# A chain of layers on 256 tokens: constant products in the waits of TensorE, and a start with its side work moved behind the first block

## The chip, the cores and the metric

The kernel runs on one core of a Trainium2 chip, as one launch. The metric is the device time of that launch in microseconds (us). Of the kernel before, three runs took 2573.61, 2573.98 and 2575.96 us; the median, 2573.98 us, is the time before. Beside the runs there is one execution that the hardware profiler recorded; all durations below are from it.

The core has five engines, each with a queue of its own that is written when the program is built: TensorE (PE in the profile, with its weight loads shown apart as PEld), VectorE (DVE), ScalarE (ACT), GpSimd (POOL) and SyncE (SP, which here only starts transfers). Transfers (DMA) are issued from the queues of SP, POOL and ACT.

## The reference

`x` is 256 tokens of 2048 features. Two blocks follow each other. Everything is float32.

```python
def mixer_a(h, w_in, w_out):                     # first layer of the first block
    q, k, v, g = jnp.split(h @ w_in, 4, axis=-1)
    o = stick_breaking_attention(heads(q), heads(k), heads(v))
    return (o * jax.nn.silu(g)) @ w_out

def residual_update(x, out, g_post, p_i, w_pp, w_pg):
    x = x + rms_norm(out, g_post)
    return x + (p_i @ w_pp) * jax.nn.sigmoid(x @ w_pg)

# first_block: layer A as above, with h = rms_norm(x, norm_pre[0]), then a layer B with latent
# attention (keys and values from one normed 512-wide latent, queries from another)

def second_block(x, c, ...):
    mod = silu(c) @ w_ada + b_ada                # 2048 x 12288: "modulation"
    sh1, sc1, gt1, sh2, sc2, gt2 = jnp.split(mod[:, None, :], 6, axis=-1)
    h = rms_norm(x, g_pre_mix) * (1.0 + sc1) + sh1
    proj = h @ w_in                              # convolution branch, attention on chosen keys, gates
    ...
    x = x + gt1 * rms_norm(mixed @ w_o, g_post_mix)
    h = rms_norm(x, g_pre_ffn) * (1.0 + sc2) + sh2
    f = (silu(h @ w_gate) * (h @ w_up)) @ w_down
    return x + gt2 * rms_norm(f, g_post_ffn)
```

## The kernel before

**Blocks and units.** The program is one long row of blocks. A `Block` computes `act(t) @ w` for up to 512 columns of a weight matrix, for both halves t0 and t1 of the tokens (128 each), in a PSUM tile per half. Its weights come in pieces: a piece is one 128-row chunk in the first block and two in nearly all others. One piece against one half of the tokens is a unit; the emission clock of the program, `u`, counts units. The float32 product is made of three float32r products per chunk: L268 (high part of the weights times high part of the activations), L269 (low part of the weights) and L270 (low part of the activations).

**The weight stream.** SP starts the transfer of each piece into one of 4 staging buffers `wst` (L122 to L132). `consume` splits it: ACT copies it to `wh` (L148), DVE makes `wl`, the remainder (L149). `wh` and `wl` have 6 ring slots; a slot is free when both halves have met the piece, and a staging buffer when its `wl` is made. Pieces are emitted some units ahead of their first product.

**Side work.** Everything else (transposing and splitting activations, norms, attention, what reads a finished sum) is in generators that `side` (L225) advances between units; `yield n` lets n units pass. This fixes the order of each engine's queue when the program is built.

**The start** (`begin_a`, L510). SP loads `ident` and the eight quarters of x between the first weight pieces. PE transposes the gain vector (`rows0`, L542), ACT copies it (`pre0`, L543). `prep` then feeds x: per 512 features of a half, four PE transposes (L363), four ACT copies with the gain (`ah`, L371), four DVE remainders (`al`, L373). The norm of x is not applied to x; `norms` sums the squares of each half (four squares, L409 on ACT, then a total on DVE, L404), POOL makes the reciprocal root (L395, L397, copies in L560 and L561: `ra`, `rqa`), and what reads a finished sum scales by it. Block q0 (the first 512 query columns) is followed by block k0. When a half of q0 is summed, `heads_t` copies it from PSUM with that scale (`nat`, L603, on ACT), PE transposes it two units later (L610) and ACT copies it out (L611). In the same stretch `rest` copies constants on DVE, transposes tables of vectors on PE (L576, L577, L587) and makes `silu_c` on ACT (L580); ACT loads an activation table there and again in L590.

**Modulation.** The 2048 x 12288 product for one row is summed on DVE in 384 chunks of 128 x 512: POOL starts the transfer of a chunk (`ast`, L245), DVE multiplies and adds (L421, L424). `spread` (L1519) gives each chunk its unit: evenly over the "calm" units, away from the turns between phases. In the kernel before they begin at unit 30.

**The turn to the second block** (`to_c`, `affine`, L1047). A quarter of a half of x at a time: normed rows (`wide`, L1091, DVE), four PE transposes (L1056), scale and shift (L1064 on DVE or L1066 on ACT), the split (`ah` L1069 on ACT, `al` L1070 on DVE). The last block of the layer before fills the time between: its t1 units (tile `sc`) stand between the transposes of t0's first and second quarter. `to_f` (from L1387, norm in L1407) does the same for the feed-forward part, through the same `affine`.

**The end.** DVE makes the last eight tiles of the output (L1480) and SP starts their transfers (L1481).

Of the kernel before, what the change touches and what calls it, by code (L numbers as in the profile page):

```python
# [16 lines left out]
AF = mybir.ActivationFunctionType  # L17
# [5 lines left out]
P = 128  # L23
# [24 lines left out]
# columns of the table of row vectors, 128 values each  # L48
# [4 lines left out]
class Act:  # L53
    """A left operand, transposed and split: hi(t, kc) + lo(t, kc) are [128 features, 128 tokens].
    `done[t]` counts the chunks of 128 features that are emitted, `gens[t]` emit the rest."""
# [7 lines left out]
class Block:  # L63
    """acc[t] = act(t) @ w[kr, c0 : c0 + n] for both halves of the tokens, then epi(t, acc[t]).
    The weights come in `np` pieces of `cp` chunks of 128 rows; `groups`: how many pieces meet one
    half of the tokens before the other; `ahead`: a pool for the first `n_ahead` pieces, which are
    then split earlier than the ring allows."""
# [22 lines left out]
class Run:  # L90
    """Weights stream in pieces of several 128-row chunks, split into two float32r parts ahead of
    the matmuls; side work is emitted between the matmuls."""
# [28 lines left out]
    # ---- the weight stream  # L121
# [57 lines left out]
    # ---- side work  # L179
# [69 lines left out]
    def go(self):  # L249
        nc = self.nc  # L250
        for b in self.blocks:
# [4 lines left out]
            for t, i in b.units():  # L256
# [17 lines left out]
                if i == b.np - 1:  # L274
# [4 lines left out]
                    # what reads the sum is emitted right behind it  # L279
# [10 lines left out]
def body(ctx, tc, a, out):  # L290
# [7 lines left out]
    # ---------------------------------------------------------------- constants and row vectors  # L298
# [38 lines left out]
    def full_act(second=False):  # L337
        """A left operand of 16 chunks; its tiles come with the first of them."""
# [12 lines left out]
    def pair_act(tiles):  # L351
        """A left operand in two tiles [128, chunks, 256 tokens]."""
# [5 lines left out]
    def feed(act, t, kc0, src, scale=None):  # L358
        """Transposes [tokens, m * 128] into chunks kc0.. of `act`; `scale`: a gain per feature."""
# [9 lines left out]
        else:  # L369
            for c in range(m):  # L370
                nc.scalar.activation(hi[:, c, :], v[:, c, :], AF.Copy, scale=scale(kc0 + c))  # L371
# [5 lines left out]
    def feed_both(act, kc0, src):  # L377
        """The same for both halves of the tokens: src[t] [tokens, 256]."""
# [13 lines left out]
    def rstd_of(pool, ss, n, post=None):  # L392
        """(ss / n + eps) ** -0.5, times `post`."""
# [17 lines left out]
    # ---------------------------------------------------------------- modulation, a bit at a time  # L411
# [49 lines left out]
    extra_pool = {}  # L461

    class Phase:
        """A pool that holds one phase's tiles."""

        def __init__(self):
            self.pool = None
# [1115 lines left out]
```

## Time and profile before

| what | value |
|---|---|
| median of 3 runs | 2573.98 us (2573.61 to 2575.96) |
| the profiled execution: its span | 2573.5 us, 0.5 us under the median |
| PE busy in the span | 2530.5 us |
| DVE, ACT, POOL busy | 1689.0, 1262.0, 291.8 us |
| moved by DMA | 562.39 MB, 219 GB/s in the mean |
| modulation chunks | 384 transfers of 256 KB, DVE 746 ns for one |

The page of the profile gives, for each engine, the time in which it executed something; registers, branches, semaphores and DMA issues are not counted. PE is busy nearly all the time, so the stretches in which it is not are what can be gained, and every instruction that is put into its queue where it would not have waited is what can be lost. In a timeline row the columns are the start, the duration, engine, line, operation, output and inputs, shapes and count; in brackets stands how long the engine sat idle before the instruction, and who released it. Merged rows ("x4") stand for several like instructions in a row.

### The profile page before, as it was taken

The page shows a single profiled execution, that of the slowest core. Times are in us where ns is not written, and L with a number is a line of the kernel's source. Part 1 is how long each engine was busy: PE and PEld are TensorE (multiplying, and loading weights), DVE is VectorE, ACT ScalarE, POOL GpSimd, SP SyncE. Part 2 cuts the span into 40 slices and gives each one's busy share as a digit, 9 for nine tenths or more (in the row PEclk, how much of TensorE's full clock was granted, in tenths as well). Part 3 has the DMA queues.
Part 4 walks back from the last instruction along what each step waited for, and adds up shares of the span by engine and source line. Part 5 has one row for each costly group of instructions (what it writes and reads, how often), then busy time and mean ns, then how long its engine had stood idle before and what let it go on. Part 6 is the DMA issues. An engine that isn't in the chain of part 4 may idle for free.

```text
span 2573.5 us, 33331 instructions
## 1 busy us (share of the span) xinstructions
PE 2530.5 (98%) x12127; PEld 2101.4 (82%) x12127; DVE 1689.0 (66%) x2304; ACT 1262.0 (49%) x1814; POOL 291.8 (11%) x561
## 2 busy tenths in 40 slices
PE   8999999999999999999999999999999999999998
PEld 6888888878889978878877877888788888888886
DVE  6666667677775566668889756676765555645545
ACT  6544464455656545554444554445544444334443
POOL 2111112111313310000000001110100100100000
PEclk9999999999999999999999999999999999999999
DMA  8777768867886566655655535875577777756553
GB/s 266 248 254 250 237 227 283 286 199 247 283 285 191 188 227 208 222 191 174 188 160 168 172 138 181 279 281 197 185 263 232 237 234 233 246 181 188 192 192 127
DMA packets 271844, 562.39 MB, mean 219 GB/s; under 512 B 20800, under 2 KB 43584, under 8 KB 269632
## 3 DMA queue, kind: packets, MB, share of 16 engines
q1 hardware_dynamic: 237264, 439.61, 52.7%
q0 software_dynamic: 34384, 120.65, 13.5%
q8 instruction: 95, 1.56, 0.2%
q14 instruction: 69, 0.57, 0.1%
q10 hardware_dynamic: 32, 0.01, 0.0%
HBM read 551.79 MB, written 8.39 MB: 218 GB/s over the span
## 4 chain that ended last, share of the span: by engine, by line
PE 93%; DVE 4%; ACT 2%; issue 1%; DMA 1%; POOL 0%; DVEq 0%; POOLq 0%; ACTq 0%; SPq 0%
PE acc L268 21%; PE acc L270 21%; PE acc L269 21%; PE sc L268 7%; PE sc L270 7%; PE sc L269 7%; PE tp L363 1%; DVE wl L149 1%; PE sc L634 1%; PE sc L984 1%; PE tp L435 1%; PE sc L1274 1%; PE sc L1240 1%; PE pv L1274 0%; PE tp L610 0%
## 5 line engine op out<-in xcount | busy, mean ns | idle before, releaser
L149 DVE TENSOR_TENSOR wl<-wst,wh 128x1024 fp32r<-128x1024 f32 (+3 forms) x794 | 949.4, 1199 | 628.7 <-ACT wh L148 627.0
L148 ACT ACTIVATE wh<-wst 128x1024 fp32r<-128x1024 f32 (+3 forms) x794 | 822.5, 1039 | 852.5 <-PE sc L270 491.2
L268 PE MATMUL acc<-wh,ah 128*128 128x512 f32 (+4 forms) x1934 | 761.5, 394 | 7.7 <-ACT wh L148 3.7
L269 PE MATMUL acc<-wl,ah 128*128 128x512 f32 (+4 forms) x1934 | 744.6, 385 | 0.9 <-DVE wl L149 0.9
L270 PE MATMUL acc<-wh,al 128*128 128x512 f32 (+4 forms) x1934 | 744.9, 385 | 0.0
L268 PEld LDWEIGHTS acc<-wh,ah 128*128 128x128 f32 x1934 | 365.1, 189 | 81.5 <-issue 6.7
L270 PEld LDWEIGHTS acc<-wh,al 128*128 128x128 f32 x1934 | 364.5, 188 | 72.3 <-DVE al L389 0.9
L269 PEld LDWEIGHTS acc<-wl,ah 128*128 128x128 f32 x1934 | 365.2, 189 | 67.3 <-DVE wl L149 2.5
L245 POOL DMA_DIRECT2D ast<-in_w_ada_dram x384 | 209.3, 545 | 1579.1 <-DVE ada L424 1391.8
L424 DVE SCALAR_TENSOR_TENSOR ada<-ast,silu_c,ada 128x512 f32<-128x512 f32 x360 | 268.7, 746 | 41.3 <-DMA ast<-in_w_ada_dram 40.5
L268 PE MATMUL sc<-wh,ah 128*128 128x512 f32 x538 | 211.5, 393 | 0.0
L270 PE MATMUL sc<-wh,al 128*128 128x512 f32 x538 | 209.6, 390 | 0.0
L269 PE MATMUL sc<-wl,ah 128*128 128x512 f32 x538 | 209.4, 389 | 0.0
L270 PEld LDWEIGHTS sc<-wh,al 128*128 128x128 f32 x538 | 101.0, 188 | 21.4
L268 PEld LDWEIGHTS sc<-wh,ah 128*128 128x128 f32 x538 | 101.0, 188 | 20.5
L269 PEld LDWEIGHTS sc<-wl,ah 128*128 128x128 f32 x538 | 101.1, 188 | 20.3
L1145 DVE SCALAR_TENSOR_TENSOR cv<-cv,wdw 128x255 f32<-128x255 f32 (+14 forms) x240 | 112.4, 468 | 6.5
L153 ACT ACTIVATE wh<-wst,cols 128x512 fp32r<-128x512 f32 (+2 forms) x112 | 68.5, 664 | 47.5 <-PE acc L270 30.5
L154 DVE SCALAR_TENSOR_TENSOR wl<-wst,cols,wh 128x512 fp32r<-128x512 f32 (+2 forms) x112 | 71.3, 681 | 25.5 <-ACT wh L153 25.3
L268 PE MATMUL acc<-wh,hh 128*128 128x512 f32 x176 | 69.3, 393 | 0.0
L268 PE MATMUL sc<-wh,hh 128*128 128x512 f32 x176 | 69.1, 392 | 0.0
L270 PE MATMUL acc<-wh,hl 128*128 128x512 f32 x176 | 68.6, 390 | 0.0
(354 smaller groups left out, 2899.1 us busy)
## 6 DMA issues: line engine op xcount, KB each, us to landing
ast<-in_w_ada_dram POOLq DMA_DIRECT2D x384, 256.0 KB, 4.2
wst<-in_w_in_dram SPq DMA_DIRECT2D x144, 512.0 KB, 3.6
wst<-in_w_in_a_dram SPq DMA_DIRECT2D x120, 512.0 KB, 4.4
wst<-in_w_gate_dram SPq DMA_DIRECT2D x88, 512.0 KB, 4.3
wst<-in_w_up_dram SPq DMA_DIRECT2D x88, 512.0 KB, 4.2
wst<-in_w_down_dram SPq DMA_DIRECT2D x88, 512.0 KB, 4.1
wst<-in_w_ple_gate_dram SPq DMA_DIRECT2D x64, 512.0 KB, 4.8
wst<-in_w_in_b_dram SPq DMA_DIRECT2D x40, 512.0 KB, 4.6
```

What stands on the lines that cost most here:

```text
L148: nc.scalar.activation(wh, st, AF.Copy)
L149: nc.vector.tensor_sub(wl, st, wh.bitcast(F32))
L153: nc.scalar.activation(wh[:, c, :], st[:, c, :], AF.Copy, scale=g)
L154: nc.vector.scalar_tensor_tensor(wl[:, c, :], st[:, c, :], g, wh[:, c, :].bitcast(F32), op0=ALU.mult, op1=ALU.subtract)
L245: self.nc.gpsimd.dma_start(st, x[1])
L268: nc.tensor.matmul(o, lhsT=hi, rhs=wh[:, c, :], start=kc == 0, stop=False)
L269: nc.tensor.matmul(o, lhsT=hi, rhs=wl[:, c, :], start=False, stop=False)
L270: nc.tensor.matmul(o, lhsT=lo, rhs=wh[:, c, :], start=False, stop=kc == b.cp * b.np - 1)
L363: nc.tensor.transpose(tp[:, c * P : (c + 1) * P], src[:, c * P : (c + 1) * P], ident)
L424: nc.vector.scalar_tensor_tensor(acc, w, s, acc, op0=ALU.mult, op1=ALU.add)
L435: nc.tensor.matmul(tp[:, c : c + 1], lhsT=acc[:, c * P : (c + 1) * P], rhs=ones, start=c == 0, stop=True, skip_group_check=True)
L1145: nc.vector.scalar_tensor_tensor(acc[:, sft:], u[:, : S - sft], wdw[:, c, k : k + 1], acc[:, sft:], op0=ALU.mult, op1=ALU.add)
```

## The change

Five things.

1. `warm(n)` puts n products of the constant matrix `mean_c` with itself (128 x 128, float32) in PE's queue, into a PSUM tile that nothing reads. There are 47: 4 + 3 + 4 around the first transposes, 10 + 6 around the first transposes of t0 in `to_c`, 10 before the first transposes of each half in `to_f`. The memset of `mean_c` on DVE moves to the top of `begin_a` for it.
2. The copy of the gain vector (`pre0`) and the first four `ah` copies move from ACT to DVE.
3. `norms` begins at unit 31 or 32 in place of 14 or 15, with one unit between squares in place of two; `rest` begins at unit 42 in place of 12. Blocks q0 and k0 sum t1 in `sc` tiles (`spare=True`) in place of `acc`, and what reads q0 waits until its scale is emitted.
4. The modulation's chunks begin at unit 140 in place of 30: the same 384 chunks on fewer units.
5. Of the last eight output transfers, the even ones go to ACT's queue.

Comments are gone too, which shifts line numbers behind L290 (feed: L370, L381, L383; `nat` L620 and its transposes L627; squares L419, total L414, `ra`/`rqa` L575/L576; `affine`'s transposes L1075).

```diff
-    def feed(act, t, kc0, src, scale=None):
+    def warm(n):
+        spin = psum_v()
+        for _ in range(n):
+            nc.tensor.matmul(spin[:, :P], lhsT=mean_c, rhs=mean_c, start=True, stop=True)
+
+    def feed(act, t, kc0, src, scale=None, first=False):
...
             for c in range(m):
-                nc.scalar.activation(hi[:, c, :], v[:, c, :], AF.Copy, scale=scale(kc0 + c))
+                if first:
+                    nc.vector.tensor_scalar(hi[:, c, :], v[:, c, :], scale(kc0 + c), None, op0=ALU.mult)
+                else:
+                    nc.scalar.activation(hi[:, c, :], v[:, c, :], AF.Copy, scale=scale(kc0 + c))
...
     def begin_a():
         st["nb"], st["hb"], st["o"] = 4, 2, None
+        nc.vector.memset(mean_c, 1.0 / 1024)
...
-        nc.vector.memset(mean_c, 1.0 / 1024)
+        warm(4)
         tp = psum_t()
         nc.tensor.transpose(tp[:, :16], rows0, ident[:16, :16])
-        nc.scalar.activation(pre0, tp[:, :16], AF.Copy)
+        nc.vector.tensor_copy(pre0, tp[:, :16])
+        warm(3)
...
-                    feed(actA, t, 4 * g, x_nat[t][...], lambda k: pre0[:, k : k + 1])
+                    feed(actA, t, 4 * g, x_nat[t][...], lambda k: pre0[:, k : k + 1],
+                         first=g == 0 and t == 0)
+                    if g == 0 and t == 0:
+                        warm(4)
...
-            yield 14 + t
+            yield 31 + t
             for g in range(4):
                 square(x_nat[t][:, g * NB : (g + 1) * NB], parts[:, g : g + 1])
-                yield 2
+                yield 1
...
         def rest():
-            yield 12
+            yield 42
...
         def epi(t, acc):
+            while t not in st["r"]:
+                yield 1
...
         add_block(wa, (0, D), j * NB, NB, actA, heads_t("qT", ...),
-                  **(dict(before=begin_a, groups=[4] * 4, cp=1, lead=4) if j == 0 else {}))
-        add_block(wa, (0, D), D + j * NB, NB, actA, heads_t("kT", ...))
+                  **(dict(before=begin_a, groups=[4] * 4, cp=1, lead=4, spare=True) if j == 0 else {}))
+        add_block(wa, (0, D), D + j * NB, NB, actA, heads_t("kT", ...), spare=j == 0)
...
         for g in range(4):
+            if g == 0 and (i or t == 0):
+                warm(10)
             tp = psum_t()
             for c in range(4):
                 nc.tensor.transpose(tp[:, c * P : (c + 1) * P], xn[g][:, c * P : (c + 1) * P], ident)
+            if g == 0 and t == i == 0:
+                warm(6)
...
-                    nc.sync.dma_start(out[0, t * P : (t + 1) * P, s2], f[:, s2])
+                    q = nc.sync if g % 2 else nc.scalar
+                    q.dma_start(out[0, t * P : (t + 1) * P, s2], f[:, s2])
...
-        for qs, us in ((range(20), calm(30, uc - 30) + calm(uc + 300, uf - 30)), (range(20, 24), calm(uf + 40, uf + 300))):
+        for qs, us in ((range(20), calm(140, uc - 30) + calm(uc + 300, uf - 30)), (range(20, 24), calm(uf + 40, uf + 300))):
```

**ACT's queue around the first norms.** In the kernel before the squares (L409) stand between the pieces of block q0 (128x512), and the last of them ahead of q0's last two pieces; the copy of q0's sum for t0 (`nat`, L603) stands behind the second piece of k0 (128x1024). This is the end of that stretch:

```order
L409 ACTIVATE junk_445,xss4_176<-wide_96 128x512
L148 ACTIVATE wh_447<-wst_340 128x512
L148 ACTIVATE wh_466<-wst_351 128x512
L148 ACTIVATE wh_472<-wst_407 128x1024
L148 ACTIVATE wh_491<-wst_427 128x1024
L603 ACTIVATE nat_509<-acc_130,rqa1_457 128x512
L148 ACTIVATE wh_515<-wst_451 128x1024
```

Now the squares (L419) stand among the last pieces of k0. Call k0's eight pieces k0.0 to k0.7. The first square of t0 follows k0.4; from the next row on, `wh_486` is k0.5, `wh_514` is k0.6 and `wh_551` is k0.7. `xss4_189` collects the sums of t0, `xss4_190` those of t1:

```order
L148 ACTIVATE wh_486<-wst_440 128x1024
L419 ACTIVATE junk_499,xss4_189<-wide_96 128x512
L419 ACTIVATE junk_501,xss4_190<-wide_97 128x512
L419 ACTIVATE junk_510,xss4_189<-wide_96 128x512
L419 ACTIVATE junk_512,xss4_190<-wide_97 128x512
L148 ACTIVATE wh_514<-wst_461 128x1024
L419 ACTIVATE junk_526,xss4_189<-wide_96 128x512
L419 ACTIVATE junk_528,xss4_190<-wide_97 128x512
L419 ACTIVATE junk_546,xss4_190<-wide_97 128x512
L620 ACTIVATE nat_548<-acc_139,rqa1_537 128x512
L148 ACTIVATE wh_551<-wst_470 128x1024
L620 ACTIVATE nat_573<-sc_235,rqa1_564 128x512
```

The fourth square of t0 is `junk_526`, behind k0.6, and the copy of q0's t1 (`nat_573`) stands behind k0.7. On DVE the total of t0 stands behind the `wl` of k0.6 and that of t1 behind the `wl` of k0.7.

**PE's queue where q0's first transposes stand.** Before, they stand in block q0 itself, two units behind the end of its t0 half (the second group, of t1, follows in k0, 18 products later):

```order
L269 MATMUL acc_221<-wl_424,ah_185 128x512
L270 MATMUL acc_221<-wh_423,al_186 128x512
L610 MATMUL tp_524<-ident_68,nat_509 128x128 x4
L268 MATMUL acc_221<-wh_447,ah_185 128x512
L269 MATMUL acc_221<-wl_448,ah_185 128x512
L270 MATMUL acc_221<-wh_447,al_186 128x512
```

Now they stand in block k0, between its third and fourth piece (`wh_457`, `wh_466`):

```order
L270 MATMUL sc_503<-wh_457,al_200 128x512
L627 MATMUL tp_581<-ident_68,nat_548 128x128 x4
L268 MATMUL acc_492<-wh_466,ah_145 128x512
L269 MATMUL acc_492<-wl_467,ah_145 128x512
L270 MATMUL acc_492<-wh_466,al_146 128x512
L268 MATMUL acc_492<-wh_466,ah_145 128x512
L269 MATMUL acc_492<-wl_467,ah_145 128x512
L270 MATMUL acc_492<-wh_466,al_146 128x512
L627 MATMUL tp_599<-ident_68,nat_573 128x128 x4
L268 MATMUL sc_503<-wh_466,ah_199 128x512
```

Counted in products (L268 to L270) from the start of the program, the two groups of four transposes stood behind 90 and 108 of them and now stand behind 132 and 138. The products themselves are the same, in the same order.

**PE's queue at `to_c`.** Before, the first transposes follow the second to last t1 pieces of the layer before directly:

```order
L269 MATMUL sc_9952<-wl_9938,ah_9355 128x512
L270 MATMUL sc_9952<-wh_9937,al_9356 128x512
L1056 MATMUL tp_10085<-ident_68,wide_10046 128x128 x4
L268 MATMUL sc_9952<-wh_9961,ah_9355 128x512
L269 MATMUL sc_9952<-wl_9962,ah_9355 128x512
```

Now 10 constant products stand ahead of them and 6 behind:

```order
L269 MATMUL sc_9920<-wl_9906,ah_9296 128x512
L270 MATMUL sc_9920<-wh_9905,al_9297 128x512
L362 MATMUL pv_10053<-mean_c_76 128x128 x10
L1075 MATMUL tp_10064<-ident_68,wide_10014 128x128 x4
L362 MATMUL pv_10069<-mean_c_76 128x128 x6
L268 MATMUL sc_9920<-wh_9929,ah_9296 128x512
L269 MATMUL sc_9920<-wl_9930,ah_9296 128x512
```

The 12 products that follow, the transposes of the second quarter behind them and the first products of the second block are as before.

More of the change, by code (lines that the diff above doesn't have):

```diff
@@ L548, in prep @@
                 for t in range(2):
-                    feed(actA, t, 4 * g, x_nat[t][:, g * NB : (g + 1) * NB], lambda k: pre0[:, k : k + 1])
+                    feed(actA, t, 4 * g, x_nat[t][:, g * NB : (g + 1) * NB], lambda k: pre0[:, k : k + 1],
+                         first=g == 0 and t == 0)
+                    if g == 0 and t == 0:
+                        warm(4)
                     yield PREP[2 * g + t]
@@ L699, in body @@
         add_block(wa, (0, D), j * NB, NB, actA, heads_t("qT", ("qT", j), lambda t: st["rq"][t]),
-                  **(dict(before=begin_a, groups=[4] * 4, cp=1, lead=4) if j == 0 else {}))
-        add_block(wa, (0, D), D + j * NB, NB, actA, heads_t("kT", ("kT", j), lambda t: st["r"][t]))
+                  **(dict(before=begin_a, groups=[4] * 4, cp=1, lead=4, spare=True) if j == 0 else {}))
+        add_block(wa, (0, D), D + j * NB, NB, actA, heads_t("kT", ("kT", j), lambda t: st["r"][t]), spare=j == 0)
         add_block(wa, (0, D), 2 * D + j * NB, NB, actA,
```

## The prediction

> **What bounds the kernel now.** I read the page first: the busy times and the chain that ended last.
>
> ```profile
> span 2573.5 us, 33331 instructions
> ...
> PE 2530.5 (98%) x12127; PEld 2101.4 (82%) x12127; DVE 1689.0 (66%) x2304; ACT 1262.0 (49%) x1814; POOL 291.8 (11%) x561
> ...
> PE 93%; DVE 4%; ACT 2%; issue 1%; DMA 1%; POOL 0%; DVEq 0%; POOLq 0%; ACTq 0%; SPq 0%
> ```
>
> PE is the bound: it stands still for 43 us of 2573.5 (2573.5 - 2530.5), and all other engines matter only where PE waits for them. So a change can gain little but those 43 us and stretches at a low clock, and what is put into PE's queue costs its own time unless PE would have stood still there. I then looked for stretches of 50 us with little PE time, with the view by windows. Its columns are PE, PEld, DVE, ACT, POOL (instructions in brackets), the granted clock, the DMA share and GB/s.
>
> ```profile
> 0.00:50.00 50.00, 40.65 (x172) 30.48 (x173) 29.23 (x69) 36.64 (x82) 16.18 (x33) 0.97 0.77 245
> 1100.00:1150.00 50.00, 46.40 (x207) 37.02 (x207) 32.78 (x48) 27.78 (x42) 2.03 (x4) 0.97 0.58 188
> 1800.00:1850.00 50.00, 44.05 (x195) 35.25 (x194) 36.24 (x59) 32.70 (x60) 5.20 (x14) 0.93 0.41 132
> ```
>
> These are the start (9.35 us idle), the turn at `to_c` (3.6) and that at `to_f` (5.95), the three places of the change; in each the clock fell too. I went through PE's timeline in each.
>
> **The start.** PE's rows there; brackets hold the idle time before and its releaser. I count products (L268 to L270) from the first at 7.15; the row at 44.08 is the 97th, that at 54.07 the 139th.
>
> ```profile
> 8.39 0.80 PE L269 MATMUL acc<-wl,ah 128*128 128x512 f32 x1 [0.45 <-DVE wl L149]
> ...
> 9.84 0.63 PE L269 MATMUL acc<-wl,ah 128*128 128x512 f32 x1
> ...
> 13.68 0.46 PE L270 MATMUL acc<-wh,al 128*128 128x512 f32 x1
> ...
> 23.34 0.63 PE L363 MATMUL tp<-ident,wide 128*128 128x128 f32 x4 [0.59 <-DVE cols L578]
> ...
> 25.95 0.43 PE L587 MATMUL tp<-ident,nat 31*128 31x31 f32 x4
> ...
> 34.76 0.50 PE L268 MATMUL acc<-wh,ah 128*128 128x512 f32 x1 [1.20 <-ACT wh L148]
> ...
> 36.92 0.50 PE L268 MATMUL acc<-wh,ah 128*128 128x512 f32 x1 [0.70 <-ACT wh L148]
> 37.65 0.78 PE L269 MATMUL acc<-wl,ah 128*128 128x512 f32 x1 [0.23 <-DVE wl L149]
> ...
> 44.08 0.39 PE L268 MATMUL acc<-wh,ah 128*128 128x512 f32 x1
> ...
> 54.07 0.39 PE L268 MATMUL acc<-wh,ah 128*128 128x512 f32 x1
> ```
>
> From 44.08 to 54.07 PE starts 42 products and four transposes (0.35 us) without a wait: 0.23 us each. Until 13.68 they are 0.43 apart, so PE is at half its clock, and so again for some 3.4 us from 37.65 on. What the change takes from this stretch, against 0.23 a product: 2.65 us of low clock up to 13.68, if the constant products wake PE; about 4.0 us of waits (23.34, 34.76 to 37.65, with the late starts around them), since ACT is rid of the squares, of two table loads and `pre0`, DVE of the copies in `rest`, and the three modulation transfers leave the weights' way; the low clock behind 37.65, 1.7 us; and 1.5 us of transposes, which move behind: a group as at 25.95 takes 0.35 us of PE's time, and there are three of `rest`'s tables (1.05) and q0's first. Together 9.85, so the 97th product comes at about 34.2.
>
> The same norms now have to be ready later in the program but earlier in time. The rows of ACT that give the prices:
>
> ```profile
> 25.54 0.64 ACT L409 ACTIVATE junk<-wide 128x512 bf16<-128x512 f32 x1
> 26.06 0.21 ACT L409 ACTIVATION_READ_ACCUMULATOR junk<-wide 128x1 f32 x1
> ...
> 39.02 1.06 ACT L148 ACTIVATE wh<-wst 128x1024 fp32r<-128x1024 f32 x1 [0.69 <-DMA wst<-in_w_in_a_dram]
> ...
> 41.47 0.69 ACT L603 ACTIVATE nat<-acc,rqa 128x512 f32<-128x512 f32 x1 [1.39 <-POOL rqa L561]
> ```
>
> POOL's part of the norm, first half and second half, and what DVE did beside the first:
>
> ```profile
> 37.76 0.55 POOL L395 TENSOR_SCALAR var<-sst 128x1 f32<-128x1 f32 x1 [24.73 <-DVE sst L404]
> 38.40 1.62 POOL L397 TENSOR_TENSOR rstd<-var,mhalf 128x1 f32<-128x1 f32 x1
> ...
> 40.34 1.09 POOL L561 TENSOR_SCALAR rqa<-rstd 128x1 f32<-128x1 f32 x1
> 41.52 0.19 POOL L395 TENSOR_SCALAR var<-sst 128x1 f32<-128x1 f32 x1
> 41.79 0.57 POOL L397 TENSOR_TENSOR rstd<-var,mhalf 128x1 f32<-128x1 f32 x1
> ...
> 42.68 0.22 POOL L561 TENSOR_SCALAR rqa<-rstd 128x1 f32<-128x1 f32 x1
> ```
> ```profile
> 37.58 2.01 DVE L149 TENSOR_TENSOR wl<-wst,wh 128x512 fp32r<-128x512 f32 x2
> ...
> 40.11 1.23 DVE L149 TENSOR_TENSOR wl<-wst,wh 128x1024 fp32r<-128x1024 f32 x1 [0.46 <-ACT wh L148]
> ```
>
> From 37.76 to 41.43 the first takes 3.7 us, beside DVE's remainders; the second takes 1.4 (41.52 to 42.90) with DVE idle. And the weights:
>
> ```profile
> wst<-in_w_in_a_dram SPq DMA_DIRECT2D x7, 512.0 KB, 4.4
> ```
>
> A transfer of k0's pieces takes 4.4 us. Now the new order. The `wl` of k0.0 ends at 41.34 before (40.11 + 1.23), some 9.9 earlier now: 31.4. That frees the staging buffer for k0.4, which lands 4.4 later with a little issue time, at about 36.2. ACT then works through its queue, in which the squares stand behind it: `wh` k0.4 to 37.3, a square (0.75 with its read) to 38.0, `wh` k0.5 to 39.1, four squares to 42.1, `wh` k0.6 to 43.2, the last square of t0 to 43.9. DVE's remainder of k0.6 ends at 44.4, the total at 44.5, POOL's part 1.4 later (DVE's next remainder is of k0.7, whose `wh` stands behind `nat`) at 45.9, `nat` at 46.6. PE has finished the 132 products ahead of q0's transposes at 34.2 + 36 x 0.23 = 42.5. **A new wait of about 4 us.** The second half follows: `wh` k0.7 to 47.6, its remainder to 48.8, total 48.9, POOL 50.3, `nat` 51.0, transposes, and the 139th product at 51.4 in place of 54.07: 2.7 us gained. Given back behind it: the tables' transposes of `rest`, 1.05 us, and a low clock after 4 us of standing still, 1.7 us as behind 37.65. **The start comes to 0.** Its bounds: -3 (no low clock) to +4 (k0.4 lands 1 us later, or DVE's remainders slow POOL once).
>
> Should the constant products not wake PE, it reaches the transposes 2.65 us later and waits so much less; the start stays at 0.
>
> **`to_c`.** First the price of a constant product, from the row of like shape (three products, f32 128x128, shown as six records), then the turn:
>
> ```profile
> 103.44 0.83 PE L634 MATMUL pv<-v,w 128*128 128x128 f32 x6
> 104.02 0.48 PE L268 MATMUL acc<-wh,ah 128*128 128x512 f32 x1
> ```
> ```profile
> 1097.98 0.60 PE L1056 MATMUL tp<-ident,wide 128*128 128x128 f32 x4
> ...
> 1106.86 0.66 PE L1056 MATMUL tp<-ident,wide 128*128 128x128 f32 x4 [2.32 <-DVE wide L1091]
> 1108.80 0.50 PE L268 MATMUL acc<-awh,ah 128*128 128x512 f32 x1 [1.28 <-ACT ah L1069]
> ```
>
> Three take 0.58 us, so one 0.193. The first transposes at 1097.98 wait for nothing. Ten products ahead of them put them off by 1.93 us, and with them the chain that ends in the waits of 1106.86 and 1108.80, since ACT and DVE there work on what these transposes give. The six behind them, 1.16 us, fit into the wait of 2.32. I take **+1.93**. Bounds: +3.1 (the six cost too) and +0.2, if PE keeps its clock: the trace has a low clock for 3.4 us behind 1108.80, 1.7 us dearer. Nearest to what is left of the waits, 1.2 and 1.28 us around the transposes, are the waits from 34.76 to 37.65 (1.20, 0.70 and 0.23 among them), after which the clock fell; so I let it fall.
>
> **`to_f`.** Two groups of ten:
>
> ```profile
> 1810.72 0.63 PE L1056 MATMUL tp<-ident,nat 128*128 128x128 f32 x4 [1.94 <-DVE nat L1407]
> ...
> 1829.59 0.60 PE L1056 MATMUL tp<-ident,nat 128*128 128x128 f32 x4
> ```
>
> Ahead of t0's transposes PE waits 1.94 us, and ten products take 1.93: 0, at most +1.9 if DVE is earlier there. Ahead of t1's it waits for nothing: **+1.93**, at least 0 if a later wait takes it up.
>
> **The rest.** The modulation's chunks come closer together:
>
> ```profile
> L245 POOL DMA_DIRECT2D ast<-in_w_ada_dram x384 | 209.3, 545 | 1579.1 <-DVE ada L424 1391.8
> L424 DVE SCALAR_TENSOR_TENSOR ada<-ast,silu_c,ada 128x512 f32<-128x512 f32 x360 | 268.7, 746 | 41.3 <-DMA ast<-in_w_ada_dram 40.5
> ```
> ```profile
> 300.00:600.00 300.00, 297.62 (x1401) 246.33 (x1400) 208.70 (x247) 154.92 (x195) 46.37 (x86) 1.00 0.75 254
> ```
>
> Some 85 of 384 chunks fall into these 300 us (POOL's 46.37 by 0.545). On fewer units the program's table puts 0.68 of a chunk on a calm unit in place of 0.55, a quarter more; 21 more chunks add 21 x 0.746 = 16 us to DVE's 208.7 and 5.5 MB to 254 GB/s (272): both keep room, and PE loses 2.4 us there in all. I cost it at 0; if that cover goes, the waits on `wl` might double a few times, +4. `spare` only changes the tile that is summed into: 0. The last transfers:
>
> ```profile
> 2564.91 2.32 SPq L1481 DMA_DIRECT2D out_dram<-wide  x4
> ```
>
> Four issues in 2.32 us, the rate at which DVE makes the tiles; the last waits for DVE, not for a queue: 0, within 0.3 either way.
>
> **Sum.** 0 + 1.93 + 0 + 1.93 + 0 = +3.9 us on the profiled span of 2573.5: 2577.4. The median of the runs lies 0.5 above that span, so the time forecast is 2577.9.
>
> **Rivals.** *The norms come later still (slower).* POOL takes 3.7 us as at 37.76 in place of 1.4, for both halves, and each adds its 2.3 to the wait, since the second half's piece k0.7 stands behind the first half's `nat`: +4.6, in all +8.5, 2582.5. It decides at whether DVE makes a remainder while POOL works. For it speaks the first norm of before, against it that the new order leaves DVE nothing to make there. The Trainium skill ("SBUF — State Buffer", on port contention) says that a DVE operation with two SBUF inputs and a GpSimd operation that reads SBUF exclude each other; the two norms above agree (1.62 against 0.57 us for the same operation), and by it the forecast's quick norm holds as long as DVE stands still.
>
> *No new wait (faster).* Were k0's pieces and the squares some 4 us earlier for t0 and t1, the start would keep its 9.85 less 1.05: -8.8, in all -4.9, 2569.1, and down to 2567.4 with a clock that holds at `to_c`. For it speaks that the squares need nothing but x, and that the first ran at 25.54 before; against it ACT's strict order: they stand behind k0.4, which has no staging buffer before 31.4.
>
> *PE keeps its clock at `to_c`.* The stretch without ordinary products shrinks there from 4.3 us (1106.86 - 2.32 = 1104.5, to 1108.80) to 3.1: -1.7, in all +2.2, 2576.2. The Trainium skill ("TensorE: Matmul & The Clock Gate", Part 1) has the clock fall after an idle window of about 3.4 us, and its Part 4 says that transposes don't count as busy in the same way; by that the 4.3 us of before had to lower the clock and 3.1 would not. The trace agrees at `to_c`, but the fall at 37.65 came with no gap over 1.4 us, against the rule, which is why I don't take it as likeliest.
>
> **Chances.** The forecast 0.42, later norms 0.20, no new wait 0.20, the clock held 0.18. A measurement can tell 0.2% of this kernel, 5.1 us, from no change. Faster by more: most of "no new wait" and a little of the clock's case, 0.20. Slower by more: "later norms" and a third of the forecast, whose 3.9 lies near the border, 0.34. Within: 0.46. The range goes from 2567.4, where nothing waits, to 2585, where the norms are late and part of the modulation's 4 us comes too.
>
> **What would show it.** In the changed kernel's profile: products 0.23 us apart from about 9 us on; the 97th near 34; a wait of 3 to 5 us at the transposes of L627, released by `nat`, and a shorter one six products on; the 139th near 51.4; POOL's root at 0.57 us in both halves; a low clock behind. At `to_c` ten constant products with no wait ahead, the wait behind them about 1.2; at `to_f` no wait where 1.94 was, and 1.93 us more ahead of t1. If L627 waits for nothing, or the modulation's transfers make the weights late in the first thousand microseconds, the prediction is wrong.

## The result and the profile after

The changed kernel takes 2600.29 us (median of 4 runs, 2599.27 to 2603.04) against 2574.97 us of the kernel before beside it: 1.01 times as long, 95% interval 1.0086 to 1.0115. The forecast was 2577.9 us with a range up to 2585. The profiled execution has a span of 2597.5 us, 24.0 more than before.

The page first. PE is busy 15.2 us longer (2545.7 - 2530.5) and idle 8.8 us longer; DVE, ACT and POOL have as much to do as before. Of the 15.2 us the 47 constant products take 14.3: the 11 at the start, at a low clock (0.43 us apart), 5.6, and the 36 others, 0.22 us apart, the rest.

```profile
span 2597.5 us, 33517 instructions
...
PE 2545.7 (98%) x12221; PEld 2116.0 (81%) x12221; DVE 1689.5 (65%) x2309; ACT 1261.5 (49%) x1809; POOL 291.6 (11%) x561
```

The products L268 to L270 are the same in the same order, so each can be looked up in both timelines of PE. The difference of its start is what was lost or won up to there (the two rows of transposes go by the transposes' own start):

| place | start before | start after | difference |
|---|---|---|---|
| behind the start | 92.67 | 92.65 | 0.0 |
| ahead of a turn in layer A's tail | 516.69 | 515.85 | -0.8 |
| behind it | 588.43 | 593.55 | +5.1 |
| ahead of a turn in layer B | 860.83 | 866.14 | +5.3 |
| behind it | 927.80 | 940.51 | +12.7 |
| ahead of B's tail | 989.89 | 1001.93 | +12.0 |
| behind it | 1027.26 | 1046.50 | +19.2 |
| `to_c`, first transposes | 1097.98 | 1119.60 | +21.6 |
| `to_f`, last product ahead of t1 | 1826.07 | 1847.83 | +21.8 |
| `to_f`, transposes of t1 | 1829.59 | 1853.62 | +24.0 |

The start gives 0 and the constant products of `to_c` and `to_f` 2.4 and 2.3 us, about as forecast. **Some 20 us more are lost in three turns between phases, places that the prediction had not looked at.** In the view by windows (PE, PEld, DVE, ACT, POOL, granted clock, DMA share, GB/s), the kernel before:

```profile
490.00:540.00 50.00, 48.62 (x232) 39.66 (x231) 34.85 (x44) 27.75 (x40) 5.11 (x9) 1.00 0.61 202
880.00:930.00 50.00, 45.70 (x253) 37.76 (x253) 23.99 (x49) 23.96 (x56) 13.65 (x26) 1.00 0.61 210
985.00:1035.00 50.00, 48.62 (x232) 39.64 (x231) 30.90 (x37) 27.50 (x37) 4.07 (x7) 1.00 0.55 183
```

And the changed kernel at about the same work:

```profile
490.00:540.00 50.00, 45.14 (x210) 36.58 (x209) 38.20 (x51) 25.37 (x39) 9.12 (x18) 0.97 0.67 221
890.00:940.00 50.00, 41.99 (x217) 33.66 (x215) 25.55 (x50) 19.56 (x45) 14.00 (x24) 0.93 0.57 199
1000.00:1050.00 50.00, 44.11 (x203) 35.60 (x202) 34.32 (x45) 23.90 (x34) 8.18 (x14) 0.93 0.65 206
```

PE has 22, 36 and 29 instructions fewer in these stretches, the clock is below 1, and in the first and third DVE and POOL have more instructions. What PE waits for shows in the second turn, read backwards from PE. First PE's wait, then ACT, DVE and POOL of the changed kernel:

```profile
906.03 0.79 PE L1001 MATMUL sc<-kT,qT 128*128 128x128 f32 x2 [5.21 <-ACT p L983]
```
```profile
905.06 0.37 ACT L982 ACTIVATE p<-sc,mx 128x128 f32<-128x128 f32 x1 [3.72 <-DVE mx L978]
```
```profile
903.74 0.75 DVE L434 SCALAR_TENSOR_TENSOR ada<-ast,silu_c,ada 128x512 f32<-128x512 f32 x1 [6.30 <-DMA ast<-in_w_ada_dram]
904.41 0.28 DVE L977 TENSOR_REDUCE mx<-sc 128x1 f32<-128x128 f32 x1
904.61 0.41 DVE L978 TENSOR_REDUCE mx<-sc 128x1 f32<-128x256 f32 x1
```
```profile
897.46 0.46 POOL L897 TENSOR_TENSOR qr<-qr,rm 128x128 f32<-128x128 f32 x1
900.53 1.67 POOL L245 DMA_DIRECT2D ast<-in_w_ada_dram  x3 [2.61 <-issue]
```

PE waits 5.2 us for the softmax on ACT, ACT for the maxima on DVE, and these stand in DVE's queue behind a chunk of the modulation (L434), which waits 6.3 us for a transfer that POOL starts only at 900.53, behind the rotation (L894 to L897). The rotation ends at 897.92; what holds POOL for the other 2.61 us the profile doesn't show. Nothing of the modulation is needed here; it merely stands ahead. At 1002 us of before it is the residual that stands behind such a chunk, and the transfers stand behind the norm on POOL:

```profile
1019.11 1.08 PE L370 MATMUL tp<-ident,x 128*128 128x128 f32 x4 [4.31 <-DVE x L755]
```
```profile
1017.56 0.75 DVE L434 SCALAR_TENSOR_TENSOR ada<-ast,silu_c,ada 128x512 f32<-128x512 f32 x1 [5.00 <-DMA ast<-in_w_ada_dram]
1018.23 1.40 DVE L755 SCALAR_TENSOR_TENSOR x<-wide,rstd,x 128x512 f32<-128x512 f32 x2
```
```profile
1010.91 1.39 POOL L407 TENSOR_TENSOR rstd<-var,mhalf 128x1 f32<-128x1 f32 x1
1012.27 1.68 POOL L245 DMA_DIRECT2D ast<-in_w_ada_dram  x3
```

In the kernel before PE takes the like transposes at 1002.74 without a wait.

**Why chunks stand there at all.** `spread` plans them for calm units only. But `side` does one step a unit: it either uses a chunk or, `elif`, loads the next. So a chunk needs two units, and the plan of 0.68 a unit can't be kept; 0.55 could not be either, but with less delay. Worked out from the program's own tables: in the kernel before, a chunk is used at most 21 units late and 23 chunks are used inside turns (where none is planned); in the changed one 46 units late and 75. And while there is a delay, a chunk is loaded one unit ahead of its use, not up to 12: 297 of 384 chunks (245 before). A unit is 6 products, some 1.4 us, and by the changed kernel's page a chunk takes 4.3 us from issue to landing. In calm stretches DVE runs ahead of PE and can wait; in a turn PE waits for DVE.

The start, in the rows that the prediction named. PE:

```profile
8.96 0.39 PE L270 MATMUL acc<-wh,al 128*128 128x512 f32 x1
...
35.02 0.39 PE L268 MATMUL acc<-wh,ah 128*128 128x512 f32 x1
...
48.56 1.12 PE L627 MATMUL tp<-ident,nat 128*128 128x128 f32 x4 [5.22 <-ACT nat L620]
...
53.01 0.66 PE L627 MATMUL tp<-ident,nat 128*128 128x128 f32 x4 [0.98 <-ACT nat L620]
53.43 0.47 PE L268 MATMUL sc<-wh,ah 128*128 128x512 f32 x1
```

ACT's first pieces behind q0 that the forecast timed (k0.4 and k0.5):

```profile
37.59 1.06 ACT L148 ACTIVATE wh<-wst 128x1024 fp32r<-128x1024 f32 x1 [0.29 <-DMA wst<-in_w_in_a_dram]
...
40.09 1.06 ACT L148 ACTIVATE wh<-wst 128x1024 fp32r<-128x1024 f32 x1 [0.83 <-DMA wst<-in_w_in_a_dram]
```

and POOL's part of the norms:

```profile
46.66 0.57 POOL L407 TENSOR_TENSOR rstd<-var,mhalf 128x1 f32<-128x1 f32 x1
...
51.13 0.57 POOL L407 TENSOR_TENSOR rstd<-var,mhalf 128x1 f32<-128x1 f32 x1
```

The 97th product starts at 35.02 (34.2 forecast, 44.08 before). The new wait at q0's transposes is 5.2 us, with a shorter one six products on, and the 139th product starts at 53.43 (51.4 forecast, 54.07 before). POOL is quick in both halves.

At `to_c` and `to_f`:

```profile
1117.37 2.39 PE L362 MATMUL pv<-mean_c 128*128 128x128 f32 x20
1119.60 0.60 PE L1075 MATMUL tp<-ident,wide 128*128 128x128 f32 x4
...
1127.14 0.39 PE L270 MATMUL acc<-awh,al 128*128 128x512 f32 x1
1128.47 0.66 PE L1075 MATMUL tp<-ident,wide 128*128 128x128 f32 x4 [0.95 <-DVE wide L1112]
1130.41 0.80 PE L268 MATMUL acc<-awh,ah 128*128 128x512 f32 x1 [1.28 <-ACT ah L1090]
1131.00 0.63 PE L269 MATMUL acc<-awl,ah 128*128 128x512 f32 x1
```
```profile
1831.04 2.39 PE L362 MATMUL pv<-mean_c 128*128 128x128 f32 x20
1833.27 0.60 PE L1075 MATMUL tp<-ident,nat 128*128 128x128 f32 x4
...
1851.39 2.39 PE L362 MATMUL pv<-mean_c 128*128 128x128 f32 x20
1853.62 0.60 PE L1075 MATMUL tp<-ident,nat 128*128 128x128 f32 x4
```

Ten products (20 records) hold the transposes back by 2.23 us (1117.37 to 1119.60). They follow ordinary products without a wait at `to_c` and ahead of t1 at `to_f`; ahead of t0 they fill the wait of 1.94. The six behind shorten the wait of 2.32 to 0.95. The clock falls all the same: the products behind 1130.41 take 0.63 us.

### The profile page after: what moved, and what is told of

Its sections match the earlier page's. It is cut to its first block, busy times and chain, and to the rows that moved or that the text cites. A ratio compares the mean times of both kernels' runs of the same rounds, so it can differ in the third digit from the quotient of the medians.

```text
span 2597.5 us, 33517 instructions
## 1 busy us (share of the span) xinstructions
PE 2545.7 (98%) x12221; PEld 2116.0 (81%) x12221; DVE 1689.5 (65%) x2309; ACT 1261.5 (49%) x1809; POOL 291.6 (11%) x561
## 4 chain that ended last, share of the span: by engine, by line
PE 91%; DVE 3%; ACT 2%; issue 1%; POOL 1%; DMA 1%; DVEq 0%; POOLq 0%; ACTq 0%
PE acc L268 20%; PE acc L270 20%; PE acc L269 20%; PE sc L268 7%; PE sc L270 7%; PE sc L269 7%; PE tp L370 1%; PE sc L651 1%; PE sc L1001 1%; DVE wl L149 1%; PE tp L445 1%; PE sc L1295 1%; DMA ast<-in_w_ada_dram 1%; ACT wh L148 1%; PE sc L1261 1%
## 5 line engine op out<-in xcount | busy, mean ns | idle before, releaser
L268 PE MATMUL acc<-wh,ah 128*128 128x512 f32 (+4 forms) x1902 | 747.1, 393 | 3.0 <-ACT wide L1349 2.4
L269 PE MATMUL acc<-wl,ah 128*128 128x512 f32 (+4 forms) x1902 | 730.3, 384 | 1.7 <-DVE wl L149 1.6
L270 PE MATMUL acc<-wh,al 128*128 128x512 f32 (+4 forms) x1902 | 730.8, 384 | 0.0
L268 PEld LDWEIGHTS acc<-wh,ah 128*128 128x128 f32 x1902 | 358.3, 188 | 73.8 <-issue 6.7
L270 PEld LDWEIGHTS acc<-wh,al 128*128 128x128 f32 x1902 | 357.6, 188 | 70.8 <-DVE al L399 0.9
L269 PEld LDWEIGHTS acc<-wl,ah 128*128 128x128 f32 x1902 | 358.4, 188 | 66.4 <-DVE wl L149 2.9
L434 DVE SCALAR_TENSOR_TENSOR ada<-ast,silu_c,ada 128x512 f32<-128x512 f32 x360 | 269.3, 748 | 51.0 <-DMA ast<-in_w_ada_dram 50.8
L268 PE MATMUL sc<-wh,ah 128*128 128x512 f32 x570 | 225.2, 395 | 0.0
L270 PE MATMUL sc<-wh,al 128*128 128x512 f32 x570 | 222.6, 391 | 0.0
L269 PE MATMUL sc<-wl,ah 128*128 128x512 f32 x570 | 222.4, 390 | 0.0
L270 PEld LDWEIGHTS sc<-wh,al 128*128 128x128 f32 x570 | 107.3, 188 | 22.8
L268 PEld LDWEIGHTS sc<-wh,ah 128*128 128x128 f32 x570 | 107.3, 188 | 21.9 <-issue 0.3
L269 PEld LDWEIGHTS sc<-wl,ah 128*128 128x128 f32 x570 | 107.4, 188 | 21.4
L268 PE MATMUL acc<-wh,hh 128*128 128x512 f32 x176 | 69.2, 393 | 0.0
L268 PE MATMUL sc<-wh,hh 128*128 128x512 f32 x176 | 69.1, 392 | 0.0
L270 PE MATMUL acc<-wh,hl 128*128 128x512 f32 x176 | 68.6, 390 | 0.0
```

What stands on the lines that cost most here:

```text
L268: nc.tensor.matmul(o, lhsT=hi, rhs=wh[:, c, :], start=kc == 0, stop=False)
L269: nc.tensor.matmul(o, lhsT=hi, rhs=wl[:, c, :], start=False, stop=False)
L270: nc.tensor.matmul(o, lhsT=lo, rhs=wh[:, c, :], start=False, stop=kc == b.cp * b.np - 1)
L434: nc.vector.scalar_tensor_tensor(acc, w, s, acc, op0=ALU.mult, op1=ALU.add)
```

## The experiments

All times are medians, with the ratio to the kernel before run beside them and its 95% interval.

**Is it the modulation, and is it its lateness?** Four runs. The edits, each alone.

e1_ada60, on the changed kernel:

```diff
-        for qs, us in ((range(20), calm(140, uc - 30) + calm(uc + 300, uf - 30)), (range(20, 24), calm(uf + 40, uf + 300))):
+        for qs, us in ((range(20), calm(60, uc - 30) + calm(uc + 300, uf - 30)), (range(20, 24), calm(uf + 40, uf + 300))):
```

e2_before_ada140, on the kernel before:

```diff
-        for qs, us in ((range(20), calm(30, uc - 30) + calm(uc + 300, uf - 30)), (range(20, 24), calm(uf + 40, uf + 300))):
+        for qs, us in ((range(20), calm(140, uc - 30) + calm(uc + 300, uf - 30)), (range(20, 24), calm(uf + 40, uf + 300))):
```

e3_two_steps, on the changed kernel, and e4_before_two_steps, the same on the kernel before:

```diff
-        elif (self.xd < len(self.extra) and self.xd - self.xc < XBUF and self.extra[self.xd][0] - 12 <= self.u):
+        if (self.xd < len(self.extra) and self.xd - self.xc < XBUF and self.extra[self.xd][0] - 12 <= self.u):
```

> The changed kernel with one number put back most of the way: the modulation's chunks begin at unit 60 in place of 140 (at 30, as before the change, silu_c would not be made yet). Theory A (spill): side work does one step a unit, either the load of a chunk or its use, so at most one chunk in two units; 320 chunks planned at 0.68 a unit run up to 46 units late and 75 of them are used inside the turns between phases (23 before the change), where POOL and DVE, each in order, hold the norms and the residual behind a chunk. At unit 60 the program's table gives 36 uses inside turns: 2578 to 2584 us. Theory B (density: DVE and DMA are too full at 0.68 a unit, wherever the chunks stand): the density falls to 0.58, nearer to 0.55 of before: 2578 to 2586. Theory C (the 20 us come from elsewhere, e.g. the constant products or spare tiles): stays at 2597 to 2602.

> The kernel before with that one number changed: chunks from unit 140 in place of 30, nothing else. Theory A and B: slower by about the 20 us that the traces show at 522, 897 and 1002 us: 2590 to 2598. Theory C: no change, 2573 to 2578.

> The changed kernel with chunks still from unit 140, but a unit may both use a chunk and load the next one (elif made if in the side work). By the program's table no chunk is late then and none is used inside a turn; the density stays 0.68 a unit. Theory A: the 20 us go, and with them some of what the 23 spilled chunks cost before: 2573 to 2580. Theory B: stays slow, 2592 to 2602. Theory C: 2597 to 2602.

> The kernel before with only that rule changed (a unit may use one chunk and load another); chunks from unit 30 as before. No chunk is used inside a turn, where 23 were. Theory A: a little faster than before, by what those 23 cost: 2566 to 2573. Theory B: no change, 2573 to 2576. Theory C says nothing.

| run | us | ratio to before |
|---|---|---|
| e1_ada60 | 2586.63 | 1.0045 (1.003 to 1.006) |
| e2_before_ada140 | 2596.32 | 1.008 (1.0065 to 1.0095) |
| e3_two_steps | 2585.52 | 1.0038 (1.0023 to 1.0053) |
| e4_before_two_steps | 2577.1 | 1.0009 (1.0 to 1.0019) |

The one number in the kernel before costs 22 us by itself; theory C (constant products or `sc` tiles) falls. With the density left at 0.68 a unit but no chunk late, 14.8 of the 25 us go (2600.29 to 2585.52), which theory B (density) can't explain. The three turns of e3_two_steps show it:

```profile
490.00:540.00 50.00, 48.62 (x232) 39.67 (x231) 36.16 (x47) 27.74 (x40) 6.95 (x13) 1.00 0.65 214
890.00:940.00 50.00, 46.16 (x241) 37.36 (x240) 23.92 (x45) 21.36 (x46) 8.14 (x16) 1.00 0.57 204
1000.00:1050.00 50.00, 48.62 (x228) 39.61 (x227) 35.47 (x43) 29.69 (x40) 5.90 (x10) 1.00 0.60 195
```

PE is busy there as it was before the change. So theory A holds for the turns. Its numbers were too good, though. e3 was to reach 2573 to 2580 and stands 11 us over the kernel before: 4 to 5 of them are the constant products (measured below), 1 the start, and the rest, 5 to 6 us, comes in small steps: in the trace 1.2 us in all between 92 and 986 us and some 3.5 between 1111 and 1684 (times of the kernel before). Of these, 1.3 us come at 1404, where PE waits for ACT and the clock falls behind the wait; e4 has that step too (1.4), and so has e11 below (1.4), whose edit touches only the start, while in the kernel before and in the changed one the clock holds there. So this step belongs to the execution and not to the chunks. The kernel before, and e11 at the same product:

```profile
1403.52 0.50 PE L268 MATMUL acc<-wh,ah 128*128 128x512 f32 x1 [2.40 <-ACT wide L1328]
```
```profile
1402.93 0.80 PE L268 MATMUL acc<-wh,ah 128*128 128x512 f32 x1 [2.18 <-ACT wide L1341]
```

What the other steps are made of was not taken apart, and for them theory B is not excluded. e4 gained nothing where I had expected 1 to 8 us: freeing the 23 chunks that the kernel before has in turns is worth nothing that can be measured. e1 lies 2.6 us above its range; at 36 chunks inside turns it still loses 4 us at 897.

**Which part of the lateness costs?** The chunk's place in the queues, or that it is loaded too shortly ahead? The two branches were swapped, so that a due load goes first. 79 chunks are then still used inside turns, but loaded 5 units ahead.

e9_load_first is that on the changed kernel, e10_before_load_first on the kernel before:

```diff
-        if self.xc < self.xd and self.extra[self.xc][0] <= self.u:
-            x = self.extra[self.xc]
-            x[2](x[3])
-            self.xc += 1
-        elif (self.xd < len(self.extra) and self.xd - self.xc < XBUF and self.extra[self.xd][0] - 12 <= self.u):
+        if (self.xd < len(self.extra) and self.xd - self.xc < XBUF and self.extra[self.xd][0] - 12 <= self.u):
             x = self.extra[self.xd]
...
             self.xd += 1
+        elif self.xc < self.xd and self.extra[self.xc][0] <= self.u:
+            x = self.extra[self.xc]
+            x[2](x[3])
+            self.xc += 1
```

> The changed kernel with the two branches of the side step swapped: when both are due, the load of the next chunk goes before the use of an old one. Still one step a unit, and by the program's table 79 chunks are still used inside turns (75 as changed); but a chunk is then loaded 5 units ahead of its use, while as changed 297 of 384 are loaded 1 unit ahead (about 1.4 us, and a transfer takes 4.3). Theory A1 (the spilled chunks cost their DVE time and their place in the queues): 2595 to 2602, as changed. Theory A2 (what costs is DVE standing still for a transfer begun one unit before, 3 to 6 us at a time inside a turn): most of the 20 us goes, 2580 to 2588.

> The kernel before with the same swap and nothing else; there 245 of 384 chunks are loaded 1 unit ahead, but only 23 are used inside turns. A2: up to 4 us faster, 2570 to 2575, since DVE's 40 us of waiting for chunks lie almost all outside the turns, where PE has work ahead. A1: no change, 2573 to 2576.

e9 takes 2598.9 us, 1.0088 (1.0074 to 1.0101), so as long as the changed kernel; e10 2575.4, 1.0002 (0.9994 to 1.0011). By the time alone A1 would win. The traces say something else (e9's profiled execution, at a span of 2592.6 us, lies at the quick end of its runs, 2594.59 to 2600.2). In the view of waits (who waited for whom, us in total, times, longest), before, changed and e9:

```profile
DVE ada L424 <- DMA ast<-in_w_ada_dram: 40.5, 32, 4.6
```
```profile
DVE ada L434 <- DMA ast<-in_w_ada_dram: 50.8, 22, 6.3
```
```profile
DVE ada L434 <- DMA ast<-in_w_ada_dram: 9.9, 4, 4.0
DVE wide L744 <- DMA big<-in_norm_post_dram: 8.4, 2, 4.7
PE tp L370 <- DMA nat<-in_p_dram: 5.7, 2, 4.7
```

DVE's waits for chunks are mostly gone in e9, and at the three turns PE comes 17 us earlier than in the changed kernel in all (from 7.0 behind it at 520 us to 10.4 ahead at 1024). But new waits stand in their place: DVE for the gain row `big`, PE for `nat`, 4.7 us each, at the beginning of layer A's tail. POOL's queue there:

```profile
444.21 0.55 POOL L241 DMA_DIRECT2D ast<-in_w_ada_dram  x1 [2.17 <-DVE ada L434]
444.75 0.54 POOL L514 DMA_DIRECT2D big<-in_norm_post_dram  x1
445.28 1.07 POOL L735 DMA_DIRECT2D x<-in_x_dram  x2
446.93 0.55 POOL L241 DMA_DIRECT2D ast<-in_w_ada_dram  x1 [0.58 <-DVE ada L434]
447.48 1.09 POOL L817 DMA_DIRECT2D nat<-in_p_dram  x2
```

A chunk's load waits on POOL until DVE has freed its buffer, and the turn's own loads stand behind it. And some 3 us go at the end of the second stretch (1764 us of the changed kernel), where DVE waits 3.0 us for another gain row (`big`, L465). So by the traces the loss of the changed kernel at its three turns was DVE standing still for chunks loaded one unit ahead (A2), and loading them sooner moves much of it to POOL's queue; the time of e9 alone doesn't show that. Whichever of the two queues a late chunk holds, the turn pays; e3 pays neither: DVE waits for chunks as long in all, 52.7 us, but only 6.2 of them in the three stretches shown, against 16.2 in the changed kernel. In the kernel before DVE waits 40.5 us for chunks, and that costs nothing: e10 brings it down to 6.2 us and the time stays.

**What do the constant products cost, and what is the start worth?**

e5_no_mid, on the changed kernel:

```diff
-            if g == 0 and (i or t == 0):
-                warm(10)
...
-            if g == 0 and t == i == 0:
-                warm(6)
```

e6_no_start, on the changed kernel:

```diff
-        warm(4)
...
-        warm(3)
...
-                    if g == 0 and t == 0:
-                        warm(4)
```

e7_norms16, on the changed kernel:

```diff
-            yield 31 + t
+            yield 16 + t
```

e11_before_start, on the kernel before (with `warm` and the argument `first` of `feed` as in the change):

```diff
+        nc.vector.memset(mean_c, 1.0 / 1024)
...
-        nc.vector.memset(mean_c, 1.0 / 1024)
+        warm(4)
...
-        nc.scalar.activation(pre0, tp[:, :16], AF.Copy)
+        nc.vector.tensor_copy(pre0, tp[:, :16])
+        warm(3)
...
-                    feed(actA, t, 4 * g, x_nat[t][:, g * NB : (g + 1) * NB], lambda k: pre0[:, k : k + 1])
+                    feed(actA, t, 4 * g, x_nat[t][:, g * NB : (g + 1) * NB], lambda k: pre0[:, k : k + 1],
+                         first=g == 0 and t == 0)
+                    if g == 0 and t == 0:
+                        warm(4)
```

> The changed kernel without the 36 constant products at to_c and to_f; those at the start stay. Cost theory (they only take PE's time, and the clock falls at to_c all the same, as the trace after shows): 2.3 us less at to_c and 2.3 us less ahead of t1 at to_f: 4 to 5 us under the changed kernel, 2595 to 2597. Rival (they keep PE's clock): as slow or slower, 2599 to 2604.

> The changed kernel without the 11 constant products at the start; the 36 later ones stay. Theory: they do raise the clock 3 to 4 us sooner, but PE then waits for the norms, which are paced by the loads and ACT's queue and not by PE; products before 13 us stay 0.43 us apart, the wait at q0's transposes shrinks by what is lost, and the time stays within 1.5 us of the changed kernel: 2598 to 2602. Rival (a faster start carries through): 2 to 3 us slower, 2602 to 2605.

> The changed kernel with the norms of x begun at unit 16 in place of 31 (still one unit between squares), all else as changed. The squares then stand ahead of k0's pieces in ACT's queue. Theory: the wait of 5.2 us at q0's transposes and the low clock behind it go, ACT has room for the squares in block q0 since the table loads are gone: 6 to 9 us under the changed kernel, 2591 to 2595. Rival (the squares make ACT late for q0's weights, as in the kernel before): a gain under 3 us, 2597 to 2601.

> The kernel before with only the first part of the new start: the 11 constant products there, pre0 and the first four ah copies on DVE. Norms, rest, modulation and all else as before. If the faster clock carries through, 2.6 us less: 2570 to 2572. If the later waits take it up (for cols at 23 us, for wh at 34 and 37 us, both set by ACT's queue), no change: 2573 to 2576; I expect the latter.

| run | us | ratio to before |
|---|---|---|
| e5_no_mid | 2596.45 | 1.0084 (1.007 to 1.0098) |
| e6_no_start | 2601.89 | 1.0105 (1.0091 to 1.0119) |
| e7_norms16 | 2598.01 | 1.009 (1.0076 to 1.0104) |
| e11_before_start | 2575.97 | 1.0006 (0.9997 to 1.0015) |

e5: 3.8 us under the changed kernel, and in the traces 2.2 at `to_c` and 2.4 ahead of t1 at `to_f`; the cost theory. e6: 1.6 over the changed kernel, which their overlapping runs can't tell from none (2599.96 to 2604.16 against 2599.27 to 2603.04), and 0.7 in the trace. PE comes to q0's transposes 1.2 us later there and waits 4.61 us where the changed kernel waits 5.22, so the wait takes up half of what the cold start lost. e11: no change that can be told; the trace is ahead by 1.8 us at 12.8 and gives 1.4 of it back at 16.08, where PE waits 1.69 us for a transfer of x.

So twice a raised clock at the start was absorbed, in half or more, by the next waits. e7 went as the rival said, not as I did: 2.3 us. The wait of 5.22 is down to 0.69, but six squares in a row now stand ahead of a weights' copy on ACT, and PE pays for that:

```profile
31.13 0.49 PE L268 MATMUL acc<-wh,ah 128*128 128x512 f32 x1 [1.55 <-ACT wh L148]
...
35.12 0.50 PE L269 MATMUL acc<-wl,ah 128*128 128x512 f32 x1 [0.81 <-DVE wl L149]
38.63 0.66 PE L627 MATMUL tp<-ident,nat 128*128 128x128 f32 x4 [0.69 <-ACT nat L620]
```

**Together.** From the changed kernel: no constant products at `to_c` and `to_f`, chunks from unit 60 with use and load in one unit, and the norms from unit 16 (e8) or, two units between squares, from 14 as in the kernel before (e12).

The edits of e5, of e3 and of e1 are those shown; that of the norms in e12 is

```diff
-            yield 31 + t
+            yield 14 + t
             for g in range(4):
                 square(x_nat[t][:, g * NB : (g + 1) * NB], parts[:, g : g + 1])
-                yield 1
+                yield 2
```

> Four edits on the changed kernel together: no constant products at to_c and to_f, norms from unit 16, chunks from unit 60, and a unit may both use and load a chunk. If the terms add: the two-step kernel stood 11 us over the kernel before, less 4.6 for the products, less 6 to 9 for the start: 2570 to 2576, at or below the kernel before.

> As the run with both (no constant products at to_c and to_f, chunks from unit 60, use and load in one unit), but the norms placed as in the kernel before: from unit 14 or 15, two units between squares. In the run with norms from 16 six squares in a row held the weights' copies back by 4 us. Spread out they should hold them back less: 1 to 3 us under that run, 2570 to 2574.

e8 takes 2574.8 us, 0.9998 (0.9989 to 1.0006): as the kernel before. e12 takes 2571.26, 0.9987 (0.9978 to 0.9995): faster than both kernels, by 3.2 us than the one before. Its trace is ahead of the kernel before by 4.1 us at 65 us already, and keeps that. Its page has less idle PE time (2568.2 - 2530.7 = 37.5 us, 43.0 before):

```profile
PE 2530.7 (99%) x12149; PEld 2102.4 (82%) x12149; DVE 1695.7 (66%) x2309; ACT 1260.9 (49%) x1809; POOL 294.0 (11%) x561
```

## Why the prediction was wrong

- **The step that failed** is "I cost it at 0; if that cover goes, the waits on `wl` might double a few times, +4", on the modulation's chunks. The sum there weighed DVE's time and the bytes, and for these there was room but for 5 to 6 us at most, as e3 shows with the same 0.68 a unit. What I did not ask is whether the program can issue 0.68 a unit. It can't: one step a unit makes at most one chunk in two units. The row of DVE's 40.5 us of waiting for chunks, which the plan loads up to 12 units ahead, was a sign of it that I read past. The plan that the change alters is not the order that results, and the chunks left their calm units for the turns. Measured: 22 us in e2, against a bound of 4. The sentence on what would prove the forecast wrong named late weights, not late chunks.
- **The start** was right in its mechanism, and its sum came out by luck in part. The 97th product was forecast at 34.2 and came at 35.02, the wait at 4 and came at 5.2, the balance behind it at 0 and came at 0.0 (at 92.67). The 139th was forecast at 51.4 and came at 53.43: POOL, DVE and `nat` were as priced, but ACT began `wh` of k0.4 at 37.59 where I had 36.2, and k0.5 at 40.09 where I had 38.0, each held by its transfer. What is given back behind is smaller than forecast by as much, 0.6 us and not 2.75, since most of the low clock lay between the two waits. So 2.0 us less were gained than forecast and 2.1 less given back, and the two errors cancel.
- **That a cold start would change nothing** was right as far as can be told: e6 and e11 move by 1.6 and 1.5 us, within the spread of the runs.
- **"No new wait"** as a rival was wrong in its size: e7 and e12 show what remains when the norms come early, 2 to 4 us, since squares that stand earlier hold the weights' copies back.
- **`to_c` and `to_f`** were right: +1.93 twice, measured 2.4 and 2.3 in the trace and 3.8 together in e5. A constant product costs 0.22 us in a row of ten, not 0.193; the row of three was too short to price ten.
- **The clock at `to_c`** was forecast to fall and fell, but by luck in part. Between the ordinary products at 1127.14 and 1130.41 lie 3.3 us from start to start, two waits of 0.95 and 1.28 us and four transposes, and so in all six profiled executions with constant products at `to_c`. Behind this gap the clock fell in four (the changed kernel, e1, e3, e6) and held in two (e7, e9). The rival after the Trainium skill ("TensorE: Matmul & The Clock Gate", Part 1), by which a gap below about 3.4 us would not lower it, came true in these two alone. And its price of 1.7 us was wrong: where the clock holds, PE only waits for DVE at the next transposes, as in e7:

```profile
1131.34 0.66 PE L1075 MATMUL tp<-ident,wide 128*128 128x128 f32 x4 [0.46 <-DVE wide L1112]
1132.76 0.63 PE L1075 MATMUL tp<-ident,wide 128*128 128x128 f32 x4 [0.76 <-DVE wide L1112]
```

  The 13th product behind the gap starts 8.8 us after the last one ahead of it in all six, at either clock.
- **POOL** was quick, 0.57 us for the root in both halves, with DVE at rest beside it; the rival of late norms did not come.
- **`spare`, the output queues:** nothing is seen of either in the trace; behind `to_f` the difference stays at 24.0 to the end. Neither was tried alone.

## What to carry to other kernels

When a change alters a plan (a range, a density, due times), follow it through the rule that carries it out: count steps per unit and where the late ones end up, before weighing time and bytes. Work that may come at any time is harmless only where nothing waits behind it in its queue: look at what stands behind it at the places where PE waits for that engine, and how long before its use its data are fetched. And a wait of a few microseconds that is filled, or a clock that is raised, is worth little or nothing while the next wait is set by another engine; find what ends that wait first.

## What was not expected of the hardware

- A row of ten float32 products of 128 x 128 takes 2.23 us, 0.22 for each, as much as a float32r product of 128 x 512 in these rows (0.23).
- The clock of PE was full by 8.96 us where constant products ran from 1.04 on, and without them at 13.7 us in the kernel before but near 11.3 in e6: the same cold stretch ended 2 us earlier in one trace than in the other.
- The same wait may or may not cost the clock. At the place that the kernel before passes at 1404 us, PE waits 2.1 to 2.7 us for ACT in all 14 profiled executions; the clock falls behind it in eight (products 0.43 us apart in place of 0.23) and holds in six, among them the one with the longest wait, 2.71 us. So one trace can't price the clock at such a place.
- 40.5 us of DVE standing still for transfers cost the kernel before nothing that swapping the loads would win back, and 52.7 us cost e3 at most 5 to 6, while 50.8 us in fewer and longer waits cost the changed kernel some 20: where they stand decides, not their sum.
